# Seven block products for the gate and up projections of a SwiGLU, and tokens in two halves

## The chip, the cores and the metric

The kernel runs on one core of a Trainium2 chip. The time is the device time of one launch in microseconds; the median of three runs of the kernel before is 1737.6 us. The engines are PE (TensorE, its weight loads shown apart as PEld), DVE (VectorE), ACT (ScalarE), POOL (GpSimd) and SP, which here only issues DMAs.

## The reference, cut to what matters

One layer of an encoder on 1024 prompt tokens and 32 decode tokens, 1056 in all, of width 1024. All is float32.

```python
xn = rmsnorm(x, norm1_g)
z = xn @ w_in                                   # 1024 x 2304, split among five branches
# A: gated spatial mixing in blocks of 128    B: GLU, depthwise conv of 31, layer norm, swish
# C: short gated conv    D: pooled means, small linear    E: attention into 256 memory tokens
merged = sum(sigmoid(xn @ w_gate[n] + b_gate[n]) * (branch[n] @ w_branch[n]) for n in range(5))
x = x + merged @ w_out
hn = rmsnorm(x, norm2_g)
x = x + (silu(hn @ w_ffn_gate) * (hn @ w_ffn_up)) @ w_ffn_down      # 1024 -> 2816 -> 1024
y = rmsnorm(x, final_norm_g)
```

## The kernel before

Activations lie feature-major: 128 features on the partitions, tokens along the free axis. The tokens stand in three chunks, `CH` (line 21), of 384, 384 and 288 (256 prompt tokens and the 32 decode tokens).

Every large product is float32 made from two float32r parts: `split` (line 116) casts a tile on ACT to its high part, and DVE subtracts that from the tile for the low part. `product` (line 130) then runs three passes over each 128-deep slice of the contraction: high times high, high times low, low times high, all into one PSUM bank. Two of the three passes have the same weights. A chunk with eight slices takes 24 matmuls, and the three chunks of one output tile 72.

Weights come as slabs of 128 x 1024 (512 KB) in the order of a list written out by hand (`want`, line 75): `slab` (line 105) hands one out, splits the next and loads two more through the queue of SP.

The stages follow each other in program order: memory keys and values; the input projections (`project`, line 346), with attention stepped as a generator beside them; the gates (`gate`, line 683), five times eight output tiles, with other branches' DVE work as generators beside them; the out projection with the residual; and the SwiGLU. Tile, the framework, places each engine's instructions near program order; an instruction that is ready sooner may go ahead of an earlier one of its engine. It adds all waits and gives a tile any buffer of its pool that is free. SBUF holds 32 `unit` tiles of 128 x 2 x 384 and 16 of 288, and PSUM is one pool of eight banks (line 59).

The norms are found by `factors` (line 247): sums over partitions by matmuls with ones, per tile of 128 tokens, a square root refined on DVE, and a diagonal matrix that another matmul spreads over the partitions. The second norm's factor is applied to the products of gate and up, not to their input.

In the SwiGLU (lines 953 to 1010) `GROUPS` cuts the 22 tiles of the hidden width into six groups. For each tile gate and up are computed for the three chunks (`fg`, `fu`, 24 matmuls each), `swiglu` (line 939) multiplies them and splits the result `h`, and after each group `down` (line 974) adds that group's products with `w_down` to the residual `x1`, which stays in SBUF. The last group runs chunk by chunk, so that the final norm of one chunk lies beside the next chunk's products.

## Time and profile before

| | us |
|---|---|
| runs | 1737.12, 1737.6, 1739.19 (median 1737.6) |
| the profiled execution, first to last instruction (its span) | 1735.9 |
| PE busy | 1723.4 |
| weight loads busy | 1709.6 |
| DVE busy | 892.8 |
| ACT busy | 452.4 |

The profiled execution's own time is given as its span alone; the median of the runs is 1.7 us above it. PE's busy time counts a matmul from its start to the end of its results, so neighbours overlap; how fast a stream of matmuls runs is seen from the distance between starts. A row of the timeline merges equal instructions that follow each other: it starts with the first one and lasts to the end of the last.

### The profile page before, as it was taken

How to read it: one execution, taken by the hardware profiler on the slowest of the kernel's cores; microseconds unless marked ns; L12 is line 12 of the kernel's file. 1: busy time of each engine (PE TensorE's matmuls, PEld its weight loads, DVE VectorE, ACT ScalarE, POOL GpSimd, SP SyncE). 2: the span in 40 equal slices, each digit the busy share in tenths (PEclk: the TensorE clock that was granted, in tenths of full speed). 3: DMA queues.
4: the chain of work that ended last, by engine and by line, in shares of the span. 5: the costliest groups of instructions: out<-in, count | busy, mean ns of one | idle time of the engine just before them, and what ended most of it. 6: DMA issues, size and time to landing. Idle time of an engine off the chain costs nothing.

```text
span 1735.9 us, 25306 instructions
## 1 busy us (share of the span) xinstructions
PE 1723.4 (99%) x10808; PEld 1709.6 (98%) x10808; DVE 892.8 (51%) x1658; ACT 452.4 (26%) x797; POOL 12.6 (1%) x27
## 2 busy tenths in 40 slices
PE   9999999999999999999999999999999999999997
PEld 8999999999999999999999999999999999999997
DVE  7696534444579974654544453333333333333346
ACT  7554222123211222422333312212111211211222
POOL 0000000000000000000000000000000000000001
PEclk9999999999999999999999999999999999999999
DMA  8111111111111111111411111111111111111102
GB/s 301 49 38 37 38 50 49 38 49 55 44 38 37 49 49 49 37 49 49 139 48 48 37 49 49 49 49 37 37 61 37 49 49 49 50 40 40 44 25 101
DMA packets 31729, 95.29 MB, mean 55 GB/s; under 512 B 5377, under 2 KB 7361, under 8 KB 31617
## 3 DMA queue, kind: packets, MB, share of 16 engines
q1 hardware_dynamic: 28832, 91.40, 15.6%
q10 hardware_dynamic: 2688, 2.22, 0.4%
q8 instruction: 85, 1.39, 0.3%
q0 software_dynamic: 96, 0.05, 0.1%
q14 instruction: 28, 0.22, 0.0%
HBM read 88.68 MB, written 4.98 MB: 54 GB/s over the span
## 4 chain that ended last, share of the span: by engine, by line
PE 98%; DVE 1%; DMA 1%; ACT 0%; issue 0%; SPq 0%; DVEq 0%; ACTq 0%
PE pg L136 27%; PE fg L136 15%; PE fu L136 15%; PE dn L136 14%; PE z L136 11%; PE pb L136 7%; PE wo L136 5%; PE va L136 1%; PE ov L136 1%; PE fs L276 1%; DMA raw<-in_w_kv 1%; PE tp L473 0%; PE sp L782 0%; PE sc L455 0%; PE fm L259 0%; PE kv L293 0%
## 5 line engine op out<-in xcount | busy, mean ns | idle before, releaser
L136 PE MATMUL pg<-xn,hl 128*128 128x384 f32 (+1 forms) x2880 | 483.8, 323 | 0.0
L136 PEld LDWEIGHTS pg<-xn,hl 128*128 128x128 f32 x2880 | 464.8, 188 | 1.8
L136 PE MATMUL fg<-hn,hl 128*128 128x384 f32 (+1 forms) x1584 | 265.1, 323 | 0.0
L136 PE MATMUL fu<-hn,hl 128*128 128x384 f32 (+1 forms) x1584 | 264.7, 322 | 0.0
L123 ACT ACTIVATE hl<-raw 128x1024 fp32r<-128x1024 f32 (+1 forms) x150 | 154.7, 1036 | 421.2 <-PE dn L136 186.9
L136 PEld LDWEIGHTS fu<-hn,hl 128*128 128x128 f32 x1584 | 255.9, 188 | 0.0
L136 PEld LDWEIGHTS fg<-hn,hl 128*128 128x128 f32 x1584 | 255.6, 188 | 0.1
L136 PE MATMUL dn<-h,hl 128*128 128x384 f32 (+1 forms) x1584 | 255.6, 322 | 0.0
L136 PEld LDWEIGHTS dn<-h,hl 128*128 128x128 f32 x1584 | 254.0, 188 | 0.0
L124 DVE TENSOR_TENSOR hl<-raw,hl 128x1024 fp32r<-128x1024 f32 (+1 forms) x150 | 178.6, 1194 | 70.1 <-ACT hl L123 70.0
L136 PE MATMUL z<-xn,hl 128*128 128x384 f32 (+1 forms) x1152 | 193.1, 325 | 0.0
L136 PEld LDWEIGHTS z<-xn,hl 128*128 128x128 f32 x1152 | 185.7, 188 | 1.1 <-DVE d_t L629 0.4
L699 ACT ACTIVATE sg<-sg,vec 128x384 f32<-128x384 f32 (+1 forms) x120 | 70.1, 584 | 284.6 <-DVE sg L698 284.5
L978 DVE TENSOR_TENSOR x<-dn,x 128x384 f32<-128x384 f32 (+1 forms) x144 | 75.0, 523 | 126.1 <-PE dn L136 126.0
L136 PE MATMUL pb<-br,hl 128*128 128x384 f32 (+1 forms) x576 | 107.9, 322 | 0.0
L698 DVE TENSOR_TENSOR sg<-pg,r 128x384 f32<-128x384 f32 x80 | 44.5, 556 | 116.6 <-PE pg L136 115.9
L136 PEld LDWEIGHTS pb<-br,hl 128*128 128x128 f32 x576 | 95.1, 188 | 0.0
L942 DVE TENSOR_TENSOR fs<-fg,r2t 128x384 f32<-128x384 f32 (+1 forms) x66 | 34.5, 524 | 115.9 <-PE fg L136 112.2
L136 PE MATMUL wo<-mg,hl 128*128 128x384 f32 (+1 forms) x576 | 92.5, 322 | 0.0
L136 PEld LDWEIGHTS wo<-mg,hl 128*128 128x128 f32 x576 | 92.4, 188 | 0.0
L945 DVE TENSOR_TENSOR fs<-fu,fs 128x384 f32<-128x384 f32 (+1 forms) x66 | 34.6, 524 | 107.4 <-PE fu L136 107.3
L842 DVE SCALAR_TENSOR_TENSOR b_y<-b_ext,vec,b_y 128x1086 f32<-128x1086 f32 x60 | 80.5, 1342 | 0.1
(208 smaller groups left out, 1023.0 us busy)
## 6 DMA issues: line engine op xcount, KB each, us to landing
raw<-in_w_gate SPq DMA_DIRECT2D x40, 512.0 KB, 3.5
raw<-in_w_fg SPq DMA_DIRECT2D x22, 512.0 KB, 3.4
raw<-in_w_fu SPq DMA_DIRECT2D x22, 512.0 KB, 3.4
raw<-in_w_dn SPq DMA_DIRECT2D x20, 512.0 KB, 3.4
raw<-in_w_in SPq DMA_DIRECT2D x16, 512.0 KB, 3.5
x<-in_x SPq DMA_DIRECT2D x16, 384.0 KB, 7.3
raw<-in_w_branch SPq DMA_DIRECT2D x10, 512.0 KB, 3.4
raw<-in_w_out SPq DMA_DIRECT2D x8, 512.0 KB, 3.5
```

The lines of the kernel that those rows point to most:

```text
L123: nc.scalar.activation(hl[:, 0], src, AF.Copy)
L124: nc.vector.tensor_tensor(hl[:, 1], src, hl[:, 0].bitcast(F32), op=ALU.subtract)
L136: nc.tensor.matmul(ps, w(wi), x(xi), start=(i == 0), stop=(i == n - 1))
L276: nc.tensor.matmul(ps[:, t0 : t0 + n], ones[:n], diag[:n, t0 : t0 + n], start=True, stop=True)
L698: nc.vector.tensor_tensor(sg, pg, r1[c], op=ALU.mult)
L699: nc.scalar.activation(sg, sg, AF.Sigmoid, bias=col("gb", n * KT + mt))
L842: nc.vector.scalar_tensor_tensor(b_y[:, j, :LB], b_ext[:, j, k : k + LB], col("bw", 31 * j + k), b_y[:, j, :LB], op0=ALU.mult, op1=ALU.add,)
L942: nc.vector.tensor_tensor(sg, pg, r2[c], op=ALU.mult)
L945: nc.vector.tensor_tensor(sg, pu, sg, op=ALU.mult)
L978: nc.vector.tensor_tensor(dst, ps, dst, op=ALU.add)
```

## The change

The tokens now stand in two halves of 528, each of two quarters of 256 prompt and 8 decode tokens; a quarter's 264 columns are one matmul's, and a half's result takes two PSUM banks (`banks2`). PSUM is cut into four single banks and two pairs up to the end of the attention, and two single banks and three pairs from there on.

Of the SwiGLU, tile 0 is computed as before (`std_ffn`). For each of the other 21 tiles the four blocks (gate or up) x (first or second half of the contraction) are taken as a 2 x 2 matrix, as are the tokens' halves with the contraction's halves, and Strassen's scheme in Winograd's form gives both results by seven products of four slices instead of eight. `pair_parts` adds the weight blocks on DVE and splits the sums, six parts ahead; `combine` builds the token blocks once, beside tile 0; `swiglu_pair` keeps the running sums in PSUM and copies partial ones out. To add tokens of different halves, `hn` must be scaled alike, so the out projection scales by a factor from its first 256 features, and the rest of the norm's factor (`by`) is applied to the products.

All down products come after all gate and up products, in groups of 8, 8 and 6 tiles. Each `h` is stored in DRAM and loaded again, as is the residual, both through POOL's queue. The last group's weights are loaded twice, once for each half.

The rest of the diff follows from the new tokens: pieces of each half, tiles for the norms (`TOKENS`: four of 128 and two of 8 in a half), attention in 16 tiles of 128 with the decode tokens behind them, two background steps a product where there was one.

```diff
-CH = ((0, 384), (384, 384), (768, 288))
-NC = len(CH)
+NC = 2
+H = T // 2
+Q = H // 2
+QP = SEQ // 4
+QD = DEC // 4
...
-GROUPS = ((0, 2), (2, 4), (6, 4), (10, 4), (14, 4), (18, 4))
+STD = 1
+GROUPS = ((0, 8), (8, 8), (16, 6))
...
+    psum = [banks.enter_context(tc.tile_pool(name="ps1", bufs=1, space=bass.MemoryType.PSUM)), 4, 2]
+    def unit(dt, name):
+        return upool.tile([P, 2, H], dt, name=name, tag="u", bufs=32)
     def bank(name="ps"):
-        return pspool.tile([P, 512], F32, name=name, tag="ps")
+        return psum[0].tile([P, 512], F32, name=name, tag="ps", bufs=psum[1])
+    def banks2(name, n=Q):
+        return psum[0].tile([P, 2, 512], F32, name=name, tag="pd", bufs=psum[2])[:, :, :n]
...
+    def part(name):
+        return wpool.tile([P, 2, 512], F32R, name=name, tag="hl", bufs=8)
...
+    def product(ps, pairs, start=True, stop=True):
         n = len(pairs) * len(PASSES)
         i = 0
         for w, x in pairs:
             for wi, xi in PASSES:
-                nc.tensor.matmul(ps, w(wi), x(xi), start=(i == 0), stop=(i == n - 1))
+                if len(ps.shape) == 2:
+                    outs = ((ps, x(xi)),)
+                else:
+                    outs = [(ps[:, q], x(xi)[:, q * Q : q * Q + Q]) for q in range(2)]
+                for out, rhs in outs:
+                    nc.tensor.matmul(
+                        out, w(wi), rhs, start=start and i == 0, stop=stop and i == n - 1,
+                        skip_group_check=not (start and stop),
+                    )
                 i += 1
...
+    for f in range(STD):
+        want("w_fg", f)
+        want("w_fu", f)
+    state["end"] = len(slabs)
     for g, (f0, fn) in enumerate(GROUPS):
-        for f in range(f0, f0 + fn):
-            want("w_fg", f)
-            want("w_fu", f)
-        if fn == 4:
-            for i in range(4):
-                want("w_dn", g * 4 - 4 + i)
-        else:
-            for i in range(2):
-                want("w_dl", i)
-    # ---- first loads
+        for _ in range(2 if g == len(GROUPS) - 1 else 1):
+            for mt in range(KT):
+                want("w_dn", g * KT + mt, fn * P)
...
+    def factors(squares, over, tiles=TOKENS, by=None):
...
+        project(gated, att_bg, 2)
...
+    banks.close()
+    psum[:] = [
+        stage.enter_context(tc.tile_pool(name="ps2", bufs=1, space=bass.MemoryType.PSUM, reuse_waits="tile")), 2, 3
+    ]
...
+    x1_d = [dpool.tile([P, 2, H], F32, name=f"x1_d{mt}", tag=f"x1_d{mt}") for mt in range(KT)]
+    for mt in range(KT):
+        x1[mt] = unit(F32, f"x1_{mt}")
+        nc.sync.dma_start(x1[mt], a["x"][:, mt])
...
+    def scaled(c, k):
+        src = x1[k][:, c]
+        nc.vector.scalar_tensor_tensor(src, src, col("g2", k), pre[c], op0=ALU.mult, op1=ALU.mult)
+    def hn_parts(c, k):
+        hn[c][k] = unit(F32R, f"hn{c}_{k}")
+        split(hn[c][k], x1[k][:, c])
...
+            dst = x1[mt][:, c]
+            nc.vector.tensor_tensor(quarters(dst), ps, quarters(dst), op=ALU.add)
+            nc.gpsimd.dma_start(x1_d[mt][:, c], dst)
             add_square(r2[c], dst, mt == 0, "sq2")
-            if mt < 3:
-                hn[c][mt] = unit(c, F32R, f"hn{c}_{mt}")
-                split(hn[c][mt], dst, col("g2", mt))
+            if mt == 1:
+                r_pre[c], spread = factors([r2[c]], 2 * P)
+                nc.scalar.copy(quarters(pre[c]), spread())
+                keep_r = const.tile([P, len(TOKENS)], F32, name=f"r_pre{c}")
+                nc.vector.tensor_copy(keep_r, r_pre[c])
+                r_pre[c] = keep_r
+            if mt > 1:
+                for k in ((0, 1, 2) if mt == 2 else (mt,)):
+                    scaled(c, k)
+                    if k < 3:
+                        hn_parts(c, k)
             if mt == KT - 1:
                 merged[c] = None
                 for k in range(3, KT):
-                    hn[c][k] = unit(c, F32R, f"hn{c}_{k}")
-                    split(hn[c][k], x1[c][k // 2][:, k % 2], col("g2", k))
+                    hn_parts(c, k)
...
+    def std_ffn(f, bg):
+        nonlocal post
+        wg, wu = wview(slab()), wview(slab())
+        h = unit(F32, f"h{f}")
+        spread = [None] * NC
+        for c in range(NC):
+            pg, pu = banks2("fg"), banks2("fu")
+            product(pg, [(lambda i, k=k: wg(i, k), lambda i, k=k: hn[c][k][:, i]) for k in range(KT)])
+            if post is None:
+                post = []
+                spread = [factors([r2[i]], D, by=r_pre[i])[1] for i in range(NC)]
+            bg(1)
+            product(pu, [(lambda i, k=k: wu(i, k), lambda i, k=k: hn[c][k][:, i]) for k in range(KT)])
+            if spread[c] is not None:
+                nc.scalar.copy(quarters(r2[c]), spread[c]())
+                post.append(r2[c])
+            sg = temp("fs")
+            sg3 = quarters(sg)
+            nc.vector.tensor_tensor(sg3, pg, quarters(post[c]), op=ALU.mult)
+            nc.scalar.activation(sg, sg, AF.Silu)
+            nc.vector.scalar_tensor_tensor(sg, sg, -1.0, post[c], op0=ALU.mult, op1=ALU.mult)
+            nc.vector.tensor_tensor(quarters(h[:, c]), pu, sg3, op=ALU.mult)
+            bg(1)
+        nc.gpsimd.dma_start(h_d[f], h)
...
+    def combine():
+        for j in range(KT // 2):
+            lo, hi = x1[j], x1[j + KT // 2]
+            b11, b12, b21, b22 = lo[:, 0], lo[:, 1], hi[:, 0], hi[:, 1]
+            nc.vector.tensor_tensor(b11, b11, b12, op=ALU.subtract)
+            nc.vector.tensor_tensor(b12, b22, b12, op=ALU.subtract)
+            nc.vector.scalar_tensor_tensor(b22, b11, -1.0, b22, op0=ALU.mult, op1=ALU.subtract)
+            nc.vector.scalar_tensor_tensor(b21, b22, -1.0, b21, op0=ALU.mult, op1=ALU.subtract)
+            for n, src in (("x6", b22), ("x5", b11), ("x7", b12), ("t4", b21)):
+                X[n][j] = unit(F32R, f"{n}_{j}")
+                split(X[n][j], src)
+            x1[j] = x1[j + KT // 2] = None
+            yield
+    comb = runner(combine())
+    for f in range(STD):
+        std_ffn(f, comb)
+    comb.drain()
...
+    ORDER = (("a11", "b11"), ("a12", "b21"), ("s2", "x6"), ("s1", "x5"), ("s3", "x7"), ("s4", "b22"), ("a22", "t4"))
...
+    def pair_parts():
+        for p in range(len(pairs)):
+            load_pair(p)
+            wa, wb = fraws.pop(p)
+            a11, a12, a21, a22 = wa[:, :512], wa[:, 512:], wb[:, :512], wb[:, 512:]
+            src = {"a11": a11, "a12": a12, "a22": a22}
+            def add(n, one, two):
+                src[n] = fpool.tile([P, 512], F32, name=f"{n}_{p}", tag="s", bufs=3)
+                nc.vector.tensor_tensor(src[n], one, two, op=ALU.add)
+            for n, _ in ORDER:
+                if n == "s2":
+                    add("s1", a21, a22)
+                    add("s2", src["s1"], a11)
+                elif n == "s3":
+                    add("s3", a11, a21)
+                elif n == "s4":
+                    add("s4", src["s2"], a12)
+                hl = part(f"{n}_{p}")
+                split(hl, src[n])
+                if n == "s3":
+                    load_pair(p + 1)
+                yield hl
...
+    AHEAD = 6
...
+    def swiglu_pair(f, hooks):
+        a_ = banks2("sa")
+        x_ = banks2("sx")
+        t = {n: fpool.tile([P, H], F32, name=f"{n}_{f}", tag="ft", bufs=4) for n in ("u2", "p5")}
+        t["p1"] = temp(f"p1_{f}")
+        h = unit(F32, f"h{f}")
+        for step, (n, xs) in enumerate(ORDER):
+            w = ready.pop(0)
+            more()
+            if n == "s1":
+                x_ = banks2("sy")
+            dst = x_ if n in ("a12", "s1", "s4") else a_
+            product(
+                dst, [(lambda i, k=k: w[:, i, k * P : k * P + P], lambda i, k=k: X[xs][k][:, i]) for k in range(KT // 2)],
+                start=n in ("a11", "a12", "s1"), stop=n in ("a12", "s4", "a22"),
+            )
+            if n == "a11":
+                nc.scalar.copy(quarters(t["p1"]), a_)
+            elif n == "a12":
+                g = t["p1"]
+                nc.vector.tensor_tensor(quarters(g), x_, quarters(g), op=ALU.add)
+                nc.vector.tensor_tensor(g, g, post[0], op=ALU.mult)
+                nc.scalar.activation(g, g, AF.Silu)
+                nc.vector.tensor_tensor(g, g, post[0], op=ALU.mult)
+            elif n == "s2":
+                nc.scalar.copy(quarters(t["u2"]), a_)
+            elif n == "s1":
+                nc.scalar.copy(quarters(t["p5"]), x_)
+            elif n == "s3":
+                u = t["p5"]
+                nc.vector.tensor_tensor(quarters(u), a_, quarters(u), op=ALU.add)
+                nc.vector.tensor_tensor(u, u, post[1], op=ALU.mult)
+            elif n == "s4":
+                g = t["u2"]
+                nc.vector.tensor_tensor(quarters(g), x_, quarters(g), op=ALU.add)
+                nc.vector.tensor_tensor(g, g, post[1], op=ALU.mult)
+                nc.scalar.activation(g, g, AF.Silu)
+                nc.vector.tensor_tensor(h[:, 1], g, t["p5"], op=ALU.mult)
+            else:
+                nc.vector.tensor_tensor(quarters(h[:, 0]), a_, quarters(t["p1"]), op=ALU.mult)
+            if hooks:
+                hooks.get(n, lambda: None)()
+        nc.gpsimd.dma_start(h_d[f], h)
...
+            hooks = {
+                "a11": lambda: load_h(first8[:4]),
+                "a12": lambda: load_h(first8[4:]),
+                "s1": lambda: parts_ahead(),
+                "s3": lambda: split_h(first8),
+                "s4": lambda: load_x1(),
+            }
+            def parts_ahead():
+                state["end"] = len(slabs)
+                load_raw()
+                load_raw()
+                split_slab()
+        swiglu_pair(f, hooks)
...
+    def down(c, mt, w, fs):
+        ps = banks2("dn")
+        product(ps, [(lambda i, k=k: w(i, k), lambda i, f=f: hp[f, c][:, i]) for k, f in enumerate(fs)])
+        dst = x1[mt][:, c]
+        nc.vector.tensor_tensor(quarters(dst), quarters(dst), ps, op=ALU.subtract)
     for g, (f0, fn) in enumerate(GROUPS):
...
+        fs = range(f0, f0 + fn)
+        if g < len(GROUPS) - 1:
+            for mt in range(KT):
+                w = wview(slab())
+                for c in range(NC):
+                    down(c, mt, w, fs)
+                if mt == 0:
+                    nf = range(GROUPS[g + 1][0], sum(GROUPS[g + 1]))
+                    load_h(nf)
+            split_h(nf)
```

## Rows read from the trace of the kernel before

**Rows 1.** The page's head: the span, busy time by engine, the granted clock.

```profile
span 1735.9 us, 25306 instructions
PE 1723.4 (99%) x10808; PEld 1709.6 (98%) x10808; DVE 892.8 (51%) x1658; ACT 452.4 (26%) x797; POOL 12.6 (1%) x27
...
PEclk9999999999999999999999999999999999999999
```

**Rows 2.** The page's chain that ended last, by engine.

```profile
PE 98%; DVE 1%; DMA 1%; ACT 0%; issue 0%; SPq 0%; DVEq 0%; ACTq 0%
```

**Rows 3.** PE's timeline after the out projection: start us, duration us, operation, count.

```profile
953.79 4.35 PE L136 MATMUL fg<-hn,hl 128*128 128x384 f32 x24
957.98 4.36 PE L136 MATMUL fu<-hn,hl 128*128 128x384 f32 x24
962.17 0.72 PE L259 MATMUL fm<-ones,r2t 128*128 128x1 f32 x6
...
975.74 3.34 PE L136 MATMUL fu<-hn,hl 128*128 128x288 f32 x24
978.92 0.83 PE L276 MATMUL fs<-diag,ones 128*128 128x128 f32 x6
```

**Rows 4.** PE's timeline in branch A: start us, duration us, operation, count.

```profile
429.51 25.55 PE L136 MATMUL va<-hl,xn 128*128 128x256 f32 x216
454.89 5.40 PE L136 MATMUL z<-xn,hl 128*128 128x384 f32 x30
```

**Rows 5.** The page's groups: count, then busy us, mean ns, idle before.

```profile
L136 PE MATMUL pg<-xn,hl 128*128 128x384 f32 (+1 forms) x2880 | 483.8, 323 | 0.0
L136 PE MATMUL fg<-hn,hl 128*128 128x384 f32 (+1 forms) x1584 | 265.1, 323 | 0.0
```

**Rows 6.** Groups by form on VectorE and ScalarE: count, busy us, mean ns.

```profile
L978 DVE TENSOR_TENSOR x<-dn,x 128x384 f32<-128x384 f32 x96 | 53.3, 556 | 90.3 <-PE dn L136 90.3
L978 DVE TENSOR_TENSOR x<-dn,x 128x288 f32<-128x288 f32 x48 | 21.9, 457 | 35.8 <-PE dn L136 35.7
L124 DVE TENSOR_TENSOR hl<-raw,hl 128x512 fp32r<-128x512 f32 x8 | 5.2, 688 | 3.3 <-ACT hl L123 3.2
L123 ACT ACTIVATE hl<-raw 128x512 fp32r<-128x512 f32 x8 | 4.6, 623 | 3.3 <-DMA raw<-in_w_kv 3.1 <-DVE hl L124 0.2
```

**Rows 7.** Stretches: length, busy us by engine, granted clock, DMA share, GB/s.

```profile
12.00:25.00 13.00, 11.90 (x58) 10.06 (x57) 9.79 (x16) 11.84 (x23) 0.00 (x0) 1.00 1.04 397
60.00:170.00 110.00, 109.54 (x731) 103.98 (x730) 91.70 (x259) 55.20 (x149) 0.85 (x2) 1.00 0.13 40
525.00:640.00 115.00, 115.00 (x720) 115.00 (x719) 108.22 (x137) 25.70 (x39) 0.00 (x0) 1.00 0.14 47
850.00:940.00 90.00, 90.00 (x562) 90.00 (x561) 45.77 (x82) 31.38 (x59) 0.00 (x0) 1.00 0.29 101
...
1727.40:1736.00 8.60, 1.74 (x6) 1.38 (x6) 3.75 (x10) 0.00 (x0) 0.00 (x0) 0.50 0.38 137
```

**Rows 8.** Timeline at the start and the end: start us, duration us, engine, operation.

```profile
19.58 5.64 PE L136 MATMUL z<-xn,hl 128*128 128x384 f32 x31
...
1716.60 6.61 PE L136 MATMUL dn<-h,hl 128*128 128x288 f32 x48
1725.75 0.15 DVE L264 TENSOR_SCALAR fv<-fm 32x1 f32<-32x1 f32 x1 [1.67 <-PE fm L259]
1727.04 0.62 DVE L271 TENSOR_SCALAR diag<-ident,fr 128x128 f32<-128x128 f32 x3
1729.18 3.49 DVE L932 SCALAR_TENSOR_TENSOR x<-x,vec,fs 128x288 f32<-128x288 f32 x8 [1.52 <-PE fs L276]
```

**Rows 9.** DMA issues: queue, count, KB each, median us to landing.

```profile
b_ext<-in_st_b POOLq DMA_DIRECT2D x1, 30.0 KB, 3.2
```

More of the change, by code (lines that the diff above doesn't have):

```diff
@@ L93, in split_slab @@
         state["split"] += 1
-        if i == len(slabs) - 1:
-            parts[i] = epool.tile([P, 2, 1024], F32R, name=f"hl{i}", tag="ext")
-        else:
-            parts[i] = wpool.tile([P, 2, 1024], F32R, name=f"hl{i}", tag="hl", bufs=4)
+        width = slabs[i][2]
+        parts[i] = [part(f"hl{i}_{s}") for s in range(2)]
         raw = raws.pop(i)
-        if slabs[i][0] == "w_kv":
-            for s in (slice(0, 512), slice(512, 1024)):
-                split(parts[i][:, :, s], raw[:, s])
-        else:
-            split(parts[i], raw)
+        for s in range(2):
+            n = min(512, width - 512 * s)
+            split(parts[i][s][:, :, :n], raw[:, 512 * s : 512 * s + n])
     def slab():
@@ L107, in slab @@
         state["used"] += 1
-        while state["split"] < min(len(slabs), i + 2):
+        end = state["end"]
+        while state["split"] < min(end, i + 2):
             while state["loaded"] <= state["split"]:
@@ L111, in slab @@
             split_slab()
-        while i > 3 and state["loaded"] < min(len(slabs), state["split"] + 2):
+        while i > 3 and state["loaded"] < min(end, state["split"] + 2):
             load_raw()
@@ L128, in split @@
             )
-    def product(ps, pairs):
+    def product(ps, pairs, start=True, stop=True):
         n = len(pairs) * len(PASSES)
@@ L245, in rsqrt @@
         nc.vector.scalar_tensor_tensor(r, t, 1.5, r, op0=ALU.add, op1=ALU.mult)
-    def factors(squares, over):
-        w = squares[0].shape[-1]
-        tiles = [(t, min(P, w - t)) for t in range(0, w, P)]
+    def factors(squares, over, tiles=TOKENS, by=None):
         k = len(tiles)
@@ L254, in factors @@
         v, t, r = (small.tile([P, k], F32, name=n) for n in ("fv", "ft", "fr"))
-        last = tiles[-1][1]
-        whole = k if last == P else k - 1
-        for i, (t0, n) in enumerate(tiles):
+        last = tiles[-1][2]
+        whole = sum(n == P for _, _, n in tiles)
+        for i, (q, t0, n) in enumerate(tiles):
             for s in squares:
                 nc.tensor.matmul(
-                    ps[:n, i : i + 1], s[:, t0 : t0 + n], ones[:, 0:1], start=s is squares[0], stop=s is squares[-1]
+                    ps[:n, i : i + 1], s[:, q * Q + t0 : q * Q + t0 + n], ones[:, 0:1],
+                    start=s is squares[0], stop=s is squares[-1],
                 )
@@ L340, in trunk_kernel, with project @@
     x_parts(1)
-    load_x(2)
-    x_parts(2)
     load_constants()
-    def project(evac, bg=None, twice=False):
+    def project(evac, bg=None, steps=1):
         w = wview(slab())
         for c in range(NC):
-            ps = bank("z")
-            product(
-                ps[:, : CH[c][1]],
-                [(lambda i, k=k: w[:, i, k], lambda i, k=k: xn[c][k][:, i]) for k in range(KT)],
-            )
+            ps = banks2("z")
+            product(ps, [(lambda i, k=k: w(i, k), lambda i, k=k: xn[c][k][:, i]) for k in range(KT)])
             if bg is not None:
-                bg(2 if twice and c == 1 else 1)
-            evac(c, ps[:, : CH[c][1]])
+                bg(steps)
+            evac(c, ps)
     def runner(*gens):
@@ L387, in trunk_kernel @@
         for j in range(2):
-            ps = bank("z")[:, : CH[c][1]]
-            product(ps, [(lambda i, k=k: wq[j][:, i, k], lambda i, k=k: xn[c][k][:, i]) for k in range(KT)])
-            nc.scalar.copy(q[c][:, j], ps)
+            ps = banks2("z")
+            product(ps, [(lambda i, k=k: wq[j](i, k), lambda i, k=k: xn[c][k][:, i]) for k in range(KT)])
+            nc.scalar.copy(quarters(q[c][:, j]), ps)
     del wq
@@ new lines, in values, with values_dec @@
+                to_branch(c, pr, h, slice(0, QP), quarters(ov))
+        def values_dec(pr, pts):
+            for h in range(2):
+                ov = bank("ov")[:HD, :DEC]
+                hc = slice((2 * pr + h) * HD, (2 * pr + h + 1) * HD)
+                for m in range(2):
+                    nc.tensor.matmul(ov, cv[:, m, hc], pts[:, 2 * h + m], start=(m == 0), stop=(m == 1))
+                for c in range(NC):
+                    to_branch(c, pr, h, slice(QP, Q), quarters(ov[:, c * 2 * QD : (c + 1) * 2 * QD]))
@@ new lines, in trunk_kernel, with drop @@
+    load_pair(0)
+    for _ in range(AHEAD):
+        more()
+    def drop(n):
+        X[n] = None
+    first8 = list(range(8))
+    for p in range(len(pairs)):
+        f = p + STD
+        hooks = None
+        if p == len(pairs) - 1:
+            hooks = {
[11 more added lines that the diff above has]
+        swiglu_pair(f, hooks)
```

549 lines of the change are left out of this document (294 added, 255 removed).

## The prediction

> **What bounds the kernel now.** I read the page's first lines, then the chain of waits, then PE's timeline. TensorE is busy 1723.4 of 1735.9 us, nearly always at the full granted clock, while VectorE is busy 51% [rows 1]. The chain that ended last is 98% PE [rows 2]. So the price is the number of matmuls times the distance from one start to the next, plus the places where PE must stand still. The duration of a matmul (337 ns for 384 columns) overlaps its neighbours; the distance is read from the timeline. 24 matmuls of 384 columns start at 953.79 and their successors at 957.98: 174.6 ns each. 24 of 288 columns take 978.92 - 975.74 = 3.18 us: 132.5 ns [rows 3]. 216 of 256 columns (in branch A) take 454.89 - 429.51 = 25.38 us: 117.5 ns [rows 4]. Every matmul has a weight load of its own (10808 of each [rows 1]), although two of the three passes over a tile use the same weights, so nothing is saved where two matmuls share them.
>
> I call one 128x128 weight part against all 1056 tokens a block. Now it is 384 + 384 + 288 columns: 2 x 174.6 + 132.5 = 481.7 ns. By the code there are 384 blocks in z (16 slabs of 24), 960 in the gates (2880 matmuls, three a block [rows 5]), 240 in pb, 192 in wo, 528 in dn: 2304; and 22 x 48 = 1056 in gate and up (1584 matmuls each [rows 5]).
>
> **The change part by part.**
>
> *Four matmuls of 264 columns for a block.* No row has 264 columns. The line through 288 and 384 (0.4385 ns a column) gives 122.0 ns, the line from 256 to 288 gives 121.3; I take 121.5. The ends are the neighbours themselves, 117.5 and 132.5. A block costs 4 x 121.5 = 486.0 ns, 4.3 more; 2304 + 48 blocks (gate and up of tile 0 stay plain): +10.1 us.
>
> *Seven products for eight.* 21 tiles of gate and up cost 48 blocks each now: 23.12 us. After: 7 products x 4 k x 3 passes x 2 quarters = 168 matmuls, 20.41 us. Saved 2.71 x 21 = 56.9 us. PE's net so far is -46.8 us. As 12,936 matmuls hang on the 264-column figure, 1 ns of it is 12.9 us.
>
> One rule speaks against this part. The Trainium skill (TensorE: Matmul & The Clock Gate, Back-to-back issue gap) gives 81 ns for 128 columns and 131 for 512 in a sustained stream with weight loads. By that line 264 columns cost about 99 ns, 288 about 102 and 384 about 114, an estimate by which narrow matmuls cost almost as much as wide ones: PE's net would be 12,936 x 0.0987 - 3360 x 0.3304 = +167 us. The trace disagrees: 384 columns take 174.6 ns, 42 more than 288, and the sum goes by the rows.
>
> *What Strassen adds on the other engines.* A 528-column VectorE operation by the line through 457 ns (288) and 556 ns (384) is 705 ns; one on 512-column weight parts takes 688 [rows 6]. A pair has four sums and seven splits of weights, 11 x 0.688, and nine evictions and gate steps, 9 x 0.705: 13.9 of 20.4 us. ScalarE has seven casts of 623 ns [rows 6], three copies and two Silu of about 0.68: 7.7 us. Both lie beside PE; parts are made six products (17 us) ahead. I cost this at nothing; without that cover each microsecond of stall in a pair costs 21.
>
> *Norm factors.* Three token tiles cost PE six small matmuls for the sums (0.72 us less the last one's 0.24, over five steps: 0.10 each) and six for the spread (0.83 less 0.27, over five: 0.11) [rows 3], so 0.42 a tile. Tiles: 13 for 9 in the first norm, 12 for 9 in the second, and 12 new ones for the pre-scale in wo. That is 8 full tiles more (3.4 us) and 11 narrow ones (8 tokens) at some 0.25: +6 us, in PE's queue between products. Ends 3 and 9.
>
> *Start and end.* The first chunk of x grows from 1.57 to 2.16 MB; the stretch around z's start at 19.58 us [rows 8] is full of DMA at 397 GB/s [rows 7], so 0.59 MB are +1.5 us, taken as 2 (0 to 4). At the end PE stops at 1716.60 + 6.61 = 1723.2 and the last eight scalings take 3.49 us for 288 columns [rows 8]. With 528 columns they take 8 x 0.69 = 5.5 (+2.0); add and square at 528 columns (+0.5), sums and diagonals over six tiles for three (+1.9, what three take from 1725.75 to the diagonals' end at 1727.66) and the larger last store add some 3: +5 (3 to 7).
>
> *From wo into the pairs.* This is the first place where PE may stand still. After wo's last product (call it T) VectorE owes the second half's split: seven operations, 4.9 us. Then `combine`: 4 x 8 operations of 0.705 or a little more, 22.9; two sets of factors over six tiles, 5.6 (1.9 for three tiles [rows 8], half as much again, twice); tile 0's gate steps, 4.3; the first part, 0.7: 38 us. PE has 48 x 0.486 = 23.3 us of tile 0 and 2.5 of factors to cover that. The gap is 12 us less what is taken beforehand: in wo VectorE is busy only 45.8 of 90 us [rows 7], and the first differences (some 4 us) need only tiles ready there. So about 6 us of standing. After work that thin the granted clock is 0.50, the 1.2 GHz level (the last 8.6 us of the trace [rows 7]), so the first products after it run slower, 2 us more. I take +8, with ends 0 (parts of pair 0 go first) and 17 (nothing taken beforehand, 3 for the clock). Should the gap not come, the last combinations are late next.
>
> *Attention.* Steps beside products fall from 25 to 22, for 24 to do, so two are left for the drain, and projections turn between two pairs of banks, not eight banks. VectorE is busy 91.7 of 110 us there, and PE waits nearly nowhere (109.5) [rows 7]. An eviction queued behind two attention steps (some 5 us of VectorE) must be done before the next product but one, 5.8 us later. I take +5: one drained chain of about 4 (seven operations one behind the other at 0.4 to 0.7, an estimate), and 1 of late evictions; ends 0 and 12.
>
> *The depthwise conv beside gates 3 and 0.* VectorE is busy 108.2 of 115 us and PE still 115.0 [rows 7]. The same columns go in fewer operations, so nothing; with three pairs of banks, up to 5.
>
> *h and x through DRAM, the down products at the end.* A pair moves 1.05 MB of weights and 0.54 MB of h in 20.4 us, 78 GB/s against the 397 seen. The last pair must bring back eight h tiles, 4.3 MB (11 us at that rate), from the end of its first product on, and it has 17.5 us left. Stores and loads stand in POOL's queue, which has little else; a small load from it lands in 3.2 us [rows 9]. Down groups wait for 16 splits (11 us of VectorE) under two products of 5.83 us, first half first. I take 1 us at each of three borders: +3 (0 to 8).
>
> *Sum.* -46.8 + 6 + 2 + 5 + 8 + 5 + 3 = -17.8: the profiled 1735.9 becomes 1718.1. The median of the runs is 1737.6, 1.7 above the profile's span, so 1719.8; I say 1720.
>
> **The rivals.**
>
> *A: everything stays covered* (0.26). No stall in the three places (-16): 1704 us. For it: no stretch of the trace leaves PE waiting, even with VectorE at 94%. Against it: 38 us of VectorE work under 26 of PE's.
>
> *B: pairs wait for each other; slower* (0.13). A pair holds two or three of the three bank pairs. If its first product must wait for the last eviction of the pair before (the slot of `sa`, and not the one free since the second product), then behind the last product come the Silu chain of `s4` (three VectorE operations and one of ScalarE, 2.8 us and handovers, with one weight split of 0.7 between, under a product of 2.9) and the last multiplication: some 1.6 us a pair, 21 x 1.6 = 34 us: 1754. It is slower from 0.85 us a pair on. Against it: two bank pairs suffice at the border, and a slot that is free can be taken. The Trainium skill (Perfetto Trace Analysis, Identifying Performance Opportunities) says that the same gap repeating on the engine that should be saturated can mean that there is not enough PSUM for the next tile; before shows no such gap, so no run yet speaks for it.
>
> *C: 264 columns cost more than the line; slower* (0.08). If the columns go in steps of 32, or a quarter that starts at an odd place costs extra, 264 is priced like 288: 132.5 ns, +11 x 12.9 = 142 us: 1862. From 1.4 ns above my figure on there is no gain left. Against it: three widths lie within 1 ns of one line, though all three are multiples of 32. The rule of the Trainium skill weighed above (TensorE: Matmul & The Clock Gate, Back-to-back issue gap) is of this kind, a price that hangs little on the columns; the row of 384 columns speaks against it.
>
> *D: no product is saved* (0.01): 192 matmuls a pair, 24 x 0.1215 x 21 = 61 us more than forecast: 1781.
>
> **How the numbers follow.** The forecast has 0.52, with its own range 1709 to 1732 (the ends of its stalls do not all fall together). The range 1700 to 1742 takes in A, and leaves out B, C and a case below A. What measurement can tell is 0.2%, 3.5 us. Faster: A and most of the forecast, 0.74. Same (1734 to 1741): 0.10. Slower: B, C and the forecast's worst sums, 0.16.
>
> **What would show it.** Starts of 264-column matmuls 121.5 ns apart in all stages, 168 a pair, pairs 20.4 us apart without a gap. One gap of about 6 us on PE where tile 0's products end, released by VectorE, with the clock at 0.5 behind it. Small waits at the drain of the attention and where the down products begin. A tail of some 17 us after the last matmul. It is wrong if the starts are above 123 ns, if every pair shows the same gap, or if the gap after tile 0 is absent or over 15 us.

## The result and the profile after

The changed kernel takes 1754.3 us (1754.07 to 1757.43, 4 runs) against 1737.5 for the kernel before (4 runs): ratio 1.0100, 95% interval 1.0086 to 1.0114. The forecast was 1720 and faster; it is slower. The head and the chain of the page after:

```profile
span 1752.4 us, 31707 instructions
PE 1708.2 (97%) x13750; PEld 1688.3 (96%) x13750; DVE 1012.1 (58%) x1771; ACT 545.3 (31%) x991; POOL 40.6 (2%) x92
...
PEclk9999899999999999999998999999999999999998
...
PE 94%; DVE 3%; DMA 1%; ACT 1%; issue 0%; DVEq 0%; SPq 0%; ACTq 0%
```

Beside [rows 1, 2]: TensorE has less to do (1708.2 for 1723.4 us busy) in a longer span, is no longer 98% of the chain, and its clock line has gaps. To find the places, take the first matmul of each stage from PE's timeline in both kernels:

| stretch | before, us | after, us | change | my terms |
|---|---|---|---|---|
| start to z | 19.6 | 18.8 | -0.8 | +2 |
| z to the first gate (first norm, attention) | 152.2 | 166.0 | +13.8 | 1.0 + 1.0 + 5 |
| gates 4 and 2 | 234.6 | 239.6 | +5.0 | 2.1 |
| branch A | 102.4 | 103.0 | +0.6 | 0.6 |
| gates 3, 0, 1 (conv) | 352.6 | 363.7 | +11.1 | 3.1 + 0 |
| out projection | 92.4 | 116.0 | +23.6 | 0.8 + 4.4 |
| gate, up, down | 769.4 | 727.7 | -41.7 | -42.8 |
| last matmul to the end | 12.7 | 17.5 | +4.8 | +5 |

(My terms: the column price, the norm factors, here 4.4 + 1.0 + 0.6 by stage, and the stalls; they add up to -17.8, the changes to +16.5.) The part named in the title does what was forecast. PE's timeline after, the first products of two pairs (start us, duration us):

```profile
1390.96 3.07 PE L157 MATMUL sa<-hn,a 128*128 128x264 f32 x24
1393.87 3.07 PE L157 MATMUL sx<-hn,a 128*128 128x264 f32 x24
...
1411.36 3.07 PE L157 MATMUL sa<-hn,a 128*128 128x264 f32 x24
```

24 matmuls every 2.91 us are 121.2 ns each, and the next pair begins 20.40 us later: 20.41 was forecast, and there is no gap here. The loss stands elsewhere, most of it in the out projection. PE's timeline there (the bracket: idle before, and who ended it):

```profile
891.18 17.61 PE L157 MATMUL wo<-mg,hl 128*128 128x264 f32 x144
911.01 1.23 PE L281 MATMUL fm<-ones,r2t 128*128 128x1 f32 x12 [2.22 <-DVE r2t L347]
915.44 3.00 PE L305 MATMUL fs<-diag,ones 128*128 128x128 f32 x12 [3.20 <-DVE diag L300]
918.37 8.14 PE L157 MATMUL wo<-mg,hl 128*128 128x264 f32 x48
928.73 1.23 PE L281 MATMUL fm<-ones,r2t 128*128 128x1 f32 x12 [2.22 <-DVE r2t L347]
931.88 3.00 PE L305 MATMUL fs<-diag,ones 128*128 128x128 f32 x12 [1.92 <-DVE diag L300]
934.80 72.57 PE L157 MATMUL wo<-mg,hl 128*128 128x264 f32 x576
```

Four waits, 9.6 us. Behind the first two, 48 matmuls take 8.14 us; undisturbed ones take 6.1. What PE waits for, from the timeline of all engines of the same place:

```profile
908.83 0.71 DVE L1003 TENSOR_TENSOR x<-wo,x 128x528 f32<-128x528 f32 x1 [4.47 <-PE wo L157]
909.57 0.64 ACT L346 ACTIVATE sq<-x 128x528 f32<-128x528 f32 x1 [5.18 <-DVE x L1003]
...
910.25 0.71 DVE L347 TENSOR_TENSOR r2t<-r2t,sq 128x528 f32<-128x528 f32 x1 [0.71 <-ACT sq L346]
...
912.64 1.28 ACT L265 ACT_TABLE_LOAD   x1 [2.43 <-DVE fv L291]
913.93 0.21 ACT L265 ACTIVATE ft<-fv 128x6 f32<-128x6 f32 x1
914.18 0.19 DVE L266 RECIPROCAL fr<-ft 128x6 f32<-128x6 f32 x1 [1.61 <-ACT ft L265]
...
915.00 1.13 DVE L300 TENSOR_SCALAR diag<-ident,fr 128x128 f32<-128x128 f32 x6
```

The pre-scale's sums need the eviction (VectorE reads the finished product out of PSUM), square and addition of the product that has just ended (908.83 to 911.0); the spread needs the sums, a root, six small operations on VectorE and the first diagonal (to 915.4). Both stand in PE's queue right behind that product, ahead of the next, so PE stands with them. The Trainium skill (ScalarE: Activation LUTs, What ACT_TABLE_LOAD costs) gives a table switch 1.28 us and a drain of about 1.38. The trace shows the 1.28, and the root 0.01 us behind it. The drain it does not show: in the conv stage of the same trace a load from 710.38 to 711.66 stands between an operation that ends at 710.36 and one that starts at 711.68.

The windows of the same stretch (length; busy PE, PEld, DVE, ACT, POOL; granted clock, DMA share, GB/s) show the second price:

```profile
891.20:908.70 17.50, 17.50 (x146) 17.38 (x144) 7.96 (x13) 4.80 (x9) 1.13 (x2) 1.00 0.77 292
908.70:918.40 9.70, 4.28 (x26) 3.86 (x25) 3.53 (x15) 2.13 (x3) 0.64 (x2) 0.71 0.41 166
918.40:926.50 8.10, 8.10 (x49) 7.90 (x48) 3.56 (x5) 2.52 (x4) 0.00 (x0) 0.72 0.00 0
926.50:934.80 8.30, 4.16 (x25) 3.82 (x25) 4.18 (x16) 1.48 (x3) 0.64 (x2) 0.70 0.30 98
934.80:945.00 10.20, 10.20 (x65) 10.20 (x65) 3.65 (x6) 1.25 (x2) 0.54 (x1) 0.74 0.00 0
945.00:1007.00 62.00, 62.00 (x513) 62.00 (x512) 37.80 (x56) 18.50 (x30) 5.40 (x10) 1.00 0.25 83
```

0.71 is a mean of the two levels, 2.4 and 1.2 GHz: PE is fully busy from 918.4 to 926.5 and still slow.

### The profile page after: what moved, and what is told of

Same layout as the page of the kernel before. It is cut to its first block, busy times and chain, and to the rows that moved or that the text cites. A ratio compares the mean times of both kernels' runs of the same rounds, so it can differ in the third digit from the quotient of the medians.

```text
span 1752.4 us, 31707 instructions
## 1 busy us (share of the span) xinstructions
PE 1708.2 (97%) x13750; PEld 1688.3 (96%) x13750; DVE 1012.1 (58%) x1771; ACT 545.3 (31%) x991; POOL 40.6 (2%) x92
## 4 chain that ended last, share of the span: by engine, by line
PE 94%; DVE 3%; DMA 1%; ACT 1%; issue 0%; DVEq 0%; SPq 0%; ACTq 0%
PE pg L157 27%; PE dn L157 15%; PE sa L157 14%; PE z L157 9%; PE sy L157 7%; PE pb L157 7%; PE wo L157 6%; PE sx L157 3%; PE va L157 1%; PE fs L305 1%; PE fu L157 1%; PE fg L157 1%; PE fm L281 1%; PE ov L157 1%; DMA raw<-in_w_kv 0%
## 5 line engine op out<-in xcount | busy, mean ns | idle before, releaser
L157 PE MATMUL pg<-xn,hl 128*128 128x264 f32 x3840 | 484.7, 286 | 0.8 <-DVE e L524 0.8
L139 ACT ACTIVATE hl<-raw 128x512 fp32r<-128x512 f32 x228 | 138.8, 615 | 417.2 <-PE pg L157 173.5
L157 PE MATMUL dn<-hp,hl 128*128 128x264 f32 x2112 | 258.0, 285 | 0.0
L157 PEld LDWEIGHTS dn<-hp,hl 128*128 128x128 f32 x2112 | 257.2, 188 | 0.2
L140 DVE TENSOR_TENSOR hl<-raw,hl 128x512 fp32r<-128x512 f32 x228 | 151.6, 671 | 142.0 <-ACT hl L139 141.4
L157 PE MATMUL z<-xn,hl 128*128 128x264 f32 x1536 | 191.6, 285 | 2.7 <-ACT r L365 2.4
L157 PE MATMUL sa<-x,s 128*128 128x264 f32 x1008 | 131.2, 287 | 2.3 <-ACT p L1154 2.3
L157 PEld LDWEIGHTS sa<-x,s 128*128 128x128 f32 x1008 | 127.0, 191 | 2.5 <-ACT p L1154 2.5
L157 PE MATMUL pb<-br,hl 128*128 128x264 f32 x768 | 103.6, 284 | 0.0
L157 PE MATMUL wo<-mg,hl 128*128 128x264 f32 x768 | 98.3, 292 | 0.0
```

The source lines that it names most:

```text
L139: nc.scalar.activation(hl[:, 0], src, AF.Copy)
L140: nc.vector.tensor_tensor(hl[:, 1], src, hl[:, 0].bitcast(F32), op=ALU.subtract)
L157: nc.tensor.matmul(out, w(wi), rhs, start=start and i == 0, stop=stop and i == n - 1, skip_group_check=not (start and stop),)
```

## Experiments

**Is it the pre-scale's place in the queue?** Five versions of it, each the changed kernel with one edit (shown shortened, the comments are mine; the multiplications that use the factor move with the spread).

e1_pre_late:
```
-  if mt == 1: factors([r2[c]]); spread()                 # both right behind product (1, c)
+  if (mt, c) in ((1, 1), (2, 0)): factors([r2[1 - c]])   # sums one product later
+  if mt == 2: spread of c                                # one product after them
```


> The changed kernel with one edit: in the out projection the six sums of the pre-scale are issued one product (5.8 us) after the square they read, and the spread one product after the sums, not both right behind each other. Theory: the loss in the out projection (116.0 us after, 92.4 before, 93.3 by my price) is TensorE standing in its queue behind the factor's chain, 2.22 + 3.20 + 2.22 + 1.92 us, and the lower clock behind it. Then the out projection takes 94 to 97 us, none of these four waits is left, and the time is 1733 to 1736 us. Rival, the loss comes from the stores of x1, the later loads or the three pairs of PSUM banks: out projection still over 110 us, time 1751 or more.

Measured: 1741.7 us (10 runs, 1738.0 to 1748.7), ratio 1.0028 (1.0016 to 1.0039); out projection 104.8 us. That is 11.2 of the 23.6 us lost, and not the expected 94 to 97: the spreads still waited 0.60 and 1.79 us.

e2_pre_filled:
```
+  hold(w, c, 18)      # 18 matmuls of 264 columns that nobody reads
   r_pre[c], spread = factors([r2[c]], 2 * P)
+  hold(w, c, 26)
```


> The changed kernel with the four waits of the pre-scale filled: 18 matmuls of 264 columns whose result nobody reads ahead of the sums and 26 behind them, in both halves (88 x 0.121 = 10.7 us of work where TensorE stood for 9.6). Theory, half of the loss is the clock that falls after a wait: the factor still takes as long, but the product after it goes at 0.121 us a matmul (5.8 us for 48, 8.1 in the changed kernel), the granted clock of the out projection rises from 0.91 to 0.97 or more, and the out projection takes 106 to 109 us for 116.0: 1744 to 1748. Rival, the clock has nothing to do with the waits, the loss is the chain alone: 116 to 118 us, time 1754 to 1757.

Measured: 1744.2 us, ratio 1.0041 (1.0026 to 1.0056). With 88 useless matmuls the kernel is 10.1 us faster, and 5.8 of that stand in the out projection. Its window:

```profile
889.80:1000.00 110.20, 109.99 (x906) 109.23 (x905) 61.20 (x110) 30.89 (x52) 8.38 (x17) 1.00 0.32 115
```

At a clock of 1.00 it takes 110.2 us, with 10.7 of useless work in it: at least 5.8 of the 23.6 lost were the clock. Of the other 4.3 us some 3 stand in gates 3, 0 and 1 (363.7 us in the changed kernel, 360.7 here, with the same lines; other runs have either), so they are not the filling's.

e3_no_pre: the factor is left out, `tensor_scalar(src, src, col("g2", k), ...)` in its place.

> The changed kernel without the pre-scale: the norm's weights are multiplied in without the factor of the first 256 channels, and the whole factor comes after the products, as in the kernel before. The multiplies stay, the small matmuls, their chain and the two ScalarE copies go. Theory: the out projection takes 93 to 95 us, so 1731 to 1735, one or two us below the version with the late factors. Rival (the loss is not the factor's): over 110 us there, 1750 or more.

Measured: 1728.1 us, ratio 0.9949 (0.9933 to 0.9966), faster than expected; out projection 93.2 us (93.3 by my price of 192 blocks). That is 22.8 us less than in the changed kernel; another 3.1 went from gates 3, 0 and 1, which this edit doesn't touch (360.6 us).

The edit also shows that "must be scaled alike", in the section on the change, is too strong. The scheme only adds and subtracts, so a factor of each token can as well be applied whole behind the products, as here. The pre-scale keeps the two halves alike in size; what that is worth in accuracy no run here tells.

e5_pre_later: the spread one product later still than in e1.

> The changed kernel with the same pre-scale and all its small matmuls, the sums one product and the spread a second product further back than the evictions they need (with the spread one product after the sums two waits of 0.60 and 1.79 us stayed, because the diagonals stood in VectorE's queue behind the splits, and the out projection took 104.8 us). Theory, only the place in TensorE's queue is dear: no wait in the out projection, about 98 us (93.3 and some 5 for 48 small matmuls), 1732 to 1736. Rival, the work of the factor itself and what it brings on VectorE costs the time whatever its place: out projection over 103 us, 1740 or more.

Measured: 1740.3 us, ratio 1.0019 (1.0009 to 1.0029), out projection 104.0. My theory, a product in between is cover, failed: waits of 1.79 and 1.09 us stayed. VectorE's timeline in that run says why:

```profile
923.94 0.17 DVE L1014 COPY r_pre<-fr 128x6 f32<-128x6 f32 x1
925.82 0.69 DVE L140 TENSOR_TENSOR hl<-raw,hl 128x512 fp32r<-128x512 f32 x1 [1.71 <-ACT hl L139]
928.02 0.71 DVE L1004 TENSOR_TENSOR x<-wo,x 128x528 f32<-128x528 f32 x1 [1.51 <-PE wo L157]
928.74 0.69 DVE L140 TENSOR_TENSOR hl<-raw,hl 128x512 fp32r<-128x512 f32 x1
929.35 0.28 DVE L300 TENSOR_SCALAR diag<-ident,fr 128x128 f32<-128x128 f32 x1
```

The factor is ready at 924.1 and VectorE is idle for over 3 us; but the diagonals are queued behind the eviction at 928.02, which waits for the end of the very product that should cover them.

e9_pre_ahead: e5 with the spread ahead of that eviction.
```
   product(ps, ...)
+  if (mt, c) in ((2, 1), (3, 0)): nc.scalar.copy(quarters(pre[1 - c]), pre_spread[1 - c]())
   nc.vector.tensor_tensor(quarters(dst), ps, quarters(dst), op=ALU.add)
```


> The changed kernel with the late pre-scale of before (sums one product back, spread one more) and one line moved: the spread, with its diagonals, is issued ahead of the eviction of the product that is to cover it. In the run before the diagonals stood in VectorE's queue behind that eviction (928.02), which waits for the product's end, while VectorE was idle for 1.5 to 3 us: so the spread waited 1.79 and 1.09 us, and the clock fell. Theory (it is the place in VectorE's queue that decides, not the number of products between): no wait in the out projection, 97 to 99 us there, 1731 to 1735. Rival (48 small matmuls bring the clock down whether TensorE waits or not): no wait, but the stretch stays at 101 us or more and the granted clock in it below 0.97, 1736 to 1740.

Measured: 1733.9 us (10 runs), ratio 0.9983 (0.9973 to 0.9993): the changed kernel with its pre-scale, now faster than before. The same place in PE's timeline, and the out projection's window:

```profile
921.15 6.11 PE L157 MATMUL wo<-mg,hl 128*128 128x264 f32 x48
927.09 1.59 PE L305 MATMUL fs<-diag,ones 128*128 128x128 f32 x12
928.61 6.09 PE L157 MATMUL wo<-mg,hl 128*128 128x264 f32 x48
```
```profile
889.80:988.60 98.80, 98.80 (x818) 98.44 (x817) 59.80 (x110) 30.87 (x52) 8.37 (x17) 1.00 0.36 129
```

The same 818 matmuls as in the 116.0 us, no wait, clock 1.00: 98.8 us. The other 17.2 us were the price of the place: the waits and the slow clock behind them.

**The conv stage.** e4_conv_paced: `3 if i < 7 else 2` becomes `3 if i < 5 else 2` beside gate 0.

> The changed kernel with three conv steps beside the first 5 products of gate 0, not 7, so that the norm steps behind the conv come two at a time from the first on. Theory: of the 11.2 us that gates 3, 0 and 1 lost, 3.1 are the 264-column price, and 8 are the waits where two norm steps stand behind each other in TensorE's queue (2.78 us before the sums at 706.56, 1.96 before a spread at 734.83) with the lower clock behind them (0.96 over 80 us). The first wait goes, and with it some 5 us: 1747 to 1750. Rival, the loss is VectorE at its limit or the three pairs of banks: no change, 1753 to 1756.

Measured: 1751.2 us, ratio 1.0082 (1.0067 to 1.0097). A wait of 2.19 us took the place of the one of 2.78, the stretch took 359.8 us, and kernels with these lines unchanged have 360.6 too: the edit did next to nothing.

e10_no_conv_norm: no `lm`, `fm`, `fs` in the norm behind the conv (the means, the sums of squares and the spread on PE), and with them the root and the other small operations of that chain.

> The changed kernel with the layer norm behind the depthwise conv left out on TensorE: the sums (lm, fm) and the spreads go, VectorE and ScalarE do operations of the same size with other operands. Gates 3, 0 and 1 took 363.7 us after and 352.6 before; the 264-column price is 3.1. Theory: all the rest (5 to 8 us) is the norm's four chunks on TensorE, waits, lower clock and small matmuls, so the stretch takes 355.5 to 357 us. Rival (VectorE full beside the conv, three pairs of banks): 359 or more.

Measured: 1736.5 us, and 349.0 us for gates 3, 0 and 1, outside both expectations: I had forgotten that before pays for this norm too (352.6 - 720 x 0.4817 = 5.8 us). So the norm costs 14.7 us after and 5.8 before, and the stretch's excess of 8.0 over the column price is all there. As the chain's small VectorE operations went too, this run alone doesn't tell which engine's part of the norm it was.

e13_conv_ahead: every gate's background step ahead of the eviction, as in e9.

> The changed kernel with one move: in every gate the step that runs beside it is issued ahead of the eviction of the gate's product, not behind it. Theory: the waits in the conv's norm (2.78 us before the sums at 706.56, 1.96 before the spread at 734.83) come, as in the out projection, from small VectorE operations that stand behind evictions of the running products (the diagonals at 734.40 behind the one at 733.78); so they go, gates 3, 0 and 1 fall from 363.7 (360.6 in other runs of the same lines) to 356 to 359, the time to 1746 to 1751. Rival, the chain of the norm is simply longer than the product beside it: waits and stretch stay, 1752 to 1756.

Measured: 1754.8 us, ratio 1.0105 (1.0088 to 1.0122), stretch 364.0, a wait of 2.02 before the sums. My theory fell; the move also brought new waits, three products that start 0.94, 0.60 and 1.07 us late behind VectorE's reading of the norm's results. What I had read past, in PE's timeline of the changed kernel:

```profile
701.74 1.62 PE L157 MATMUL pb<-br,hl 128*128 128x264 f32 x12
703.19 0.59 PE L938 MATMUL lm<-bsm,ones 128*128 128x256 f32 x2
706.56 0.58 PE L281 MATMUL fm<-ones,bsm 128*128 128x1 f32 x4 [2.78 <-DVE bsm L944]
707.00 0.69 PE L305 MATMUL fs<-diag,ones 128*128 128x128 f32 x4
707.45 7.58 PE L157 MATMUL pg<-xn,hl 128*128 128x264 f32 x48
```

In the code the sums `fm` come a step later, behind the product that starts at 707.45; in the queue they stand ahead of it. The planner (Tile) had moved them. e17_conv_step (on top of e16, below) puts one more empty `yield` between `lm` and `fm` and makes the loop one step longer.

> As e16, with one more empty step between a conv chunk's means and the sums of its squares, so that the second sums stay behind a product in TensorE's queue. Theory (they had been moved ahead of that product, and the wait of 2.2 us is their place): that wait goes, gates 3, 0 and 1 fall from 361.4 to 357 to 360 us, the time from 1715.1 to 1711 to 1714. Rival, the chain takes longer than a product whatever its place: the wait stays or moves to the spread, 1714.5 to 1717.

Measured: 1709.0 us, ratio 0.9839 (0.9826 to 0.9853); e16 has 1715.1. Better than I dared:

```profile
695.37 1.61 PE L157 MATMUL pb<-br,hl 128*128 128x264 f32 x12
696.82 0.50 PE L281 MATMUL fm<-ones,bsm 128*128 128x1 f32 x4
697.18 0.68 PE L939 MATMUL lm<-bsm,ones 128*128 128x256 f32 x2
697.51 6.14 PE L157 MATMUL pg<-xn,hl 128*128 128x264 f32 x48
```

No wait is left in the conv stage, the second one (1.96 us before a spread) included, and the stretch takes 355.2 us, 2.6 over before, for 3.1 of column price. VectorE's operations and the pairs of banks are those of e16, where it takes 361.4 us.

**The attention stretch.** After the last product of this stage PE has only the drained steps (timeline of the changed kernel):

```profile
168.46 0.60 PE L507 MATMUL tp<-ident,pe 128*128 128x128 f32 x4
...
171.92 1.68 PE L482 MATMUL sd<-ckv,q_dec 64*32 64x256 f32 x4 [1.72 <-DVE mx L493]
...
181.51 0.62 PE L540 MATMUL ov<-pts,ckv 128*64 128x32 f32 x8 [1.78 <-ACT pe L495]
...
184.77 8.04 PE L157 MATMUL pg<-xn,hl 128*128 128x264 f32 x48 [0.76 <-DVE e L524]
```

e6_att_early: `project(gated, att_bg, 2 + j)` and `project(place, att_bg, 3 - j)`.

> The changed kernel with three attention steps, not two, beside the four products of the second gating and of the first pool slab, so that all 24 steps are done before the last product. Theory: the stretch from z to the first gate, 166.0 us after and 152.2 before, loses 11 us at its end, where after 168.46 no product stands between the steps and TensorE waits for each (1.72, 0.54, 1.78, 0.38, 0.76 us) and then runs at the lower clock (48 matmuls in 8.04 us). It falls to 154 to 160 us, the time to 1743 to 1749. Rival: VectorE, busy 44.8 of 50 us before, is the bound; then the waits move to the products beside which three steps stand, the stretch stays over 163 us and the time at 1752 or above.

Measured: 1744.7 us, ratio 1.0043 (1.0028 to 1.0058), 9.6 us less than the changed kernel: 7.0 in the stretch (159.0) and 2.0 in the gates behind it, whose first product runs at full clock again.

```profile
174.50 4.37 PE L157 MATMUL z<-xn,hl 128*128 128x264 f32 x34
178.71 5.99 PE L157 MATMUL pg<-xn,hl 128*128 128x264 f32 x48
```

**What the scheme itself saves.** e7_std21: `STD = 21`, the combination beside the last plain tile.

> The changed kernel with 21 of the 22 tiles of gate and up plain (two halves of 528, 192 matmuls of 264 columns) and one pair by Strassen's scheme; the combination stands beside the last plain tile. It tells what the scheme itself saves: 20 tiles of 23.3 us for 20 pairs of 20.4, +58 us, 1809 to 1815, if the saving is all there. Rival, the pairs' additions cost what the products save: 1750 to 1780.

Measured: 1814.7 us, ratio 1.0445 (1.0429 to 1.0460): 60.4 us for 20 tiles. The saving is all there.

**Together.** e8_no_pre_conv_att is e3, e4 and e6 in one.

> Three edits together: no pre-scale, the conv's steps paced as before, the attention's steps early. If the losses are three waits in different stages, they add: 1728 (without the pre-scale), less 1 to 4 (conv), less 6 to 11 (attention): 1714 to 1722, faster than both kernels. If they share a cause (VectorE's total, the clock), less than the sum: 1724 to 1728.

Measured: 1720.9 us, ratio 0.9906 (0.9891 to 0.9921): the losses add. e12_pre_ahead_att, the same with the pre-scale of e9 in place of none, took 1728.5 (just outside the expected 1724 to 1728), ratio 0.9948 (0.9933 to 0.9962); in the profiles 5.5 us of the difference to e8 stand in the out projection (99.1 for 93.6) and 3.1 in gates 3, 0 and 1. It is the fastest version measured that keeps the pre-scale. e11_no_pre_att_std2 is e8 with `STD = 2`.

> The fastest version so far (no pre-scale, attention early, 1720.9 us) with two plain tiles ahead of the pairs in place of one. A plain tile costs 2.9 us more than a pair; it gives the combination 23 us more of cover. Theory: the border from wo into the pairs still loses 2.3 + 1.5 us of waits and some 3 us by the clock; these go, so 1716 to 1719. Rival: the waits there come from the pair itself (its first parts, its banks) and stay: 1722 to 1725.

Measured: 1721.0 us. Of the waits at the border from wo into the pairs (1.52 and 2.26 us) none is left, and gate, up and down together took 2.5 us less, but the attention and conv stretches were 4 us longer in that run: no difference that can be told. e14_no_pre_att_conv_ahead and e15_and_first_norm_ahead stand on e3, e6 and the move of e13; e15 also issues the first norm's spread ahead of its product (`project(keep(1), att_bg, ahead=x_spread)`).

> No pre-scale, attention early, and the gates' steps issued ahead of the eviction. If e13's theory holds: 1720.9 less 2 to 5: 1716 to 1719. If not, 1720 to 1724.

> As e14, and the first norm's spread issued ahead of the product that it belongs to, not behind it: there the next product waits twice for ScalarE's copy of the factor (1.19 us each) and the second spread 0.95 us for VectorE. Theory: these three waits go, the stretch from z to the first gate falls from 159 to 154 to 156 us, the time 3 to 5 us below e14. Rival, the stretch is held by VectorE (busy 44.8 of 50 us there): less than 1 us.

Measured: 1726.6 and 1719.5 us. The first is worse than either view: it has the new waits of e13 (0.94, 0.59 and 1.07 us), and its stretch of gates 3, 0 and 1 takes 363.9 us for 361.4 in e8, which also paces the conv. From e14 to e15 the stretch from z falls from 159.1 to 154.7, as expected; the time falls by 7.1 us, more than the 3 to 5 expected. e16_all_behind joins that to e8, with the conv's steps behind the eviction again.

> No pre-scale, attention early, the conv's steps paced and behind the eviction as in e8, and the first norm's spread ahead of its product as in e15. Theory: e8's 1720.9 less the 4.4 us that the stretch from z to the first gate fell from e14 to e15 (159.1 to 154.7): 1715 to 1718. Rival, e15's gain over e14 (7 us) was mostly other stretches' changes from build to build: 1719 to 1722.

Measured: 1715.1 us, ratio 0.9873 (0.9857 to 0.9890). With e17's one `yield` on top, 1709.0 us is the fastest: 28 us below before, without the pre-scale. With it in e9's place that would be some 1715, an estimate from e9's 98.8 and e3's 93.2 us in the out projection; it was not run.

## Why the prediction was wrong

**The step that failed** is the one called "Norm factors", which costed the pre-scale by its matmuls, "+6 us, in PE's queue between products". The matmuls were nearly right: e9 has 98.8 us in the out projection, e3 93.2 without them, so they cost 5.6 where the term has 4.4. "Between products" was not: I took from [rows 3] that such matmuls follow each other 0.1 us apart, and did not ask what stands ahead of them here. In [rows 3] a whole product lies between a sum and its spread; in the changed code there is none, for two chains of 2.2 and 4.4 us. The place cost 17.2 us where the term had 0. That is half of the 34.3 us between the -17.8 forecast and the +16.5 measured; the next two paragraphs have most of the rest.

**The conv, forecast 0** (to 5), cost 8 us (5 in the runs that have 360.6), by the same mistake in a place that the code doesn't show: a gate has 16 products where it had 24, the norm four chunks where it had three, and the planner moved one chunk's sums ahead of the only product between. I looked for VectorE's load and bank pairs; e17, which has the same of both, shows that neither was it.

**Attention, forecast +5** (0 to 12): right in kind (steps left for the drain), too small. The drain cost 7.0 us in the stretch and 2.0 in the gates behind it by the clock (e6). Another 4.4 (e15 against e14) are not the attention's: the first norm's spread stood behind its product, and twice the next product waited 1.19 us until ScalarE had copied it out. So this is the mistake of the norm factors once more.

**Right:** 264 columns (121.2 ns), the pairs (20.40 us), the end (+4.8), the sum of gate, up and down (-41.7 for -42.8). The start came out at -0.8 for +2.

**Right in size, not in kind:** from wo into the pairs. Tile 0 and the first pair took 32.6 + 24.6 us for some 28.7 (192 matmuls, the sums and the spreads at their undisturbed pace) + 20.4 of work, which is the 8 forecast. But the forecast was one gap of about 6 us at tile 0's end and a slow clock behind it. PE's timeline has three short waits, and two products slowed (7.57 us for 6.0, 4.71 for 3.1), the first of them with no wait ahead of it:

```profile
1013.03 2.28 PE L281 MATMUL fm<-ones,r2t 128*128 128x1 f32 x24
1015.24 7.57 PE L157 MATMUL fu<-hn,hl 128*128 128x264 f32 x48
...
1024.92 6.09 PE L157 MATMUL fg<-hn,hl 128*128 128x264 f32 x48 [0.69 <-ACT r2t L1040]
...
1039.78 3.17 PE L157 MATMUL sa<-hn,a 128*128 128x264 f32 x24 [1.52 <-DVE fs L1044]
...
1048.12 4.71 PE L157 MATMUL sa<-x,s 128*128 128x264 f32 x24 [2.26 <-ACT p L1154]
```

That these add up to 8 is luck.

**The rivals.** B gave 1754 us, the measured number, and is wrong: it put 1.6 us into each of 21 pairs, but only the first pair has a wait of that size (2.26 us, for ScalarE's copy of its first result); in the other 20 there is one of 0.38 us. The rule about repeating gaps that was weighed there (the Trainium skill, Perfetto Trace Analysis, Identifying Performance Opportunities) finds none to apply to. A right number is no evidence for a mechanism; the timeline is. A (1704) was nearer to what the scheme can give: with the rest of the small work in its place and the pre-scale left out e17 takes 1709.

**The range** left out any case in which small new work waits in the queue of the engine that sets the time, because I had priced that work by its duration alone.

## What to carry to other kernels

Price a small operation on the bounding engine by its place in two queues: what it needs must be ready when its turn comes, and what makes it ready must not be queued behind an eviction of the product that is to cover it. Read that place from the trace, since a planner may have moved it from where the code has it. Allow for a slow clock behind each such wait: here it cost at least 5.8 us in the out projection, and 0 to 3 in the conv.

## What was not expected of the hardware

Waits of only 2 to 3 us can bring TensorE to its 1.2 GHz level for the work behind them: after 2.22 + 3.20 us, with 12 one-column matmuls between, 48 matmuls took 8.14 us for 6.1. Work that nobody reads, put into the waits, held the clock at 1.00 and made the out projection 5.8 us shorter.

Nor is the fall regular. The same lines of gates 3, 0 and 1, with the same waits (2.77 and 1.95 us), took 363.7 us in some runs, with a clock of 0.94 around the waits, and 360.6 in others, with 1.00. And a wait is not needed for it: behind the second norm's 24 one-column sums, which PE runs without a pause, 48 matmuls took 7.57 us in the changed kernel (shown above) and 6.10 in e3:

```profile
987.52 2.28 PE L281 MATMUL fm<-ones,r2t 128*128 128x1 f32 x24
989.73 6.10 PE L157 MATMUL fu<-hn,hl 128*128 128x264 f32 x48
```

What decides between the two no run here shows.
